# A two-layer decoder trunk: the order of row tiles in paired FFN blocks, the DRAM round trips of x, and the place of a bias table

## The chip, the cores and the metric

The kernel runs on one core of one Trainium2 chip. The metric is the device time of one launch in microseconds, for the slowest (here the only) core. Five engines work side by side, each through its own list of instructions in order, and wait for each other by semaphores: TensorE (PE, with its weight loads as PEld), VectorE (DVE), ScalarE (ACT), GpSimd (POOL) and SyncE (SP). DMAs are issued by SP and by POOL.

## The reference

For a sequence of 256 rows of width 2048, two layers run one after the other. Cut to what matters here:

```python
for i in range(2):
    h = rmsnorm(x, norm_mix[i])
    x = x + (even_mixer if i == 0 else odd_mixer)(h)      # attention-like heads and an output projection
    h = rmsnorm(x, norm_ffn[i])
    x = x + (silu(h @ ffn_gate[i]) * (h @ ffn_up[i])) @ ffn_down[i]          # inner width 5632
    x = x + sigmoid(x @ ple_gate[i]) * (p[i] @ ple_proj[i])                  # "ple" below
return rmsnorm(x, final_norm)
```

The odd mixer adds a bias to its logits, `t5_table[t5_bucket(distance)]`, one column for each of 16 heads. The kernel makes it once as a table `toep` of 128 x 16 x 256.

## The kernel before, in words

**Products.** Each weight matrix is read from DRAM in row tiles of 256 rows by 512 columns (512 KB; the tile `raw`). A row tile is split into two float32r parts: ACT writes the high part `whi` (L197), DVE subtracts it from the original to get the low part `wlo` (L199). The activations lie transposed in two big buffers, A and B, each with a high and a low part (`Ah`, `Al`, `Bh`, `Bl`). A plain row tile is 12 matmuls of 512 columns (lines 352, 353, 355: high times high, high times `wlo`, low times high, for two blocks of 128 rows of the weights and two halves of the sequence). Only the second of each three needs `wlo`.

**Pairs.** In the FFN two column blocks, a and b, are computed together. Four row tiles of the pair are replaced by seven "quads" of 6 matmuls each (lines 421 to 423), whose operands are sums of weight quarters (`e`, `keys`; added by DVE at L385) and sums of activations (`sums`, in the tile `tabs`). What is split there is split at L180 (ACT) and L182 (DVE). Some products land in a PSUM tile `at` and are combined by DVE (L431 to L435); when a block is finished DVE adds two such results to its accumulator (L441, L442, called close below). The order of work within a pair is a string: a digit is a quad, `a` or `b` a plain row tile of that block. In `"1a3a7a6a2aab5b4bbbb"`, quad 7 needs two DVE sums, quads 6 and 4 one each.

**The order of everything.** `run` walks through the list of row tiles. Before the products of row tile i it records the splits up to tile i+3 (`LOOK = 3`; four buffers for `whi` and `wlo`); after them, what becomes of a finished block; then one step of each background job that is due (`background`). One row tile is one tick. A job that yields `None, 7` is asked again 7 ticks later; `after=[...]` holds a job back until other jobs are done; `need` forces a job's steps when a product wants its result. DMA issues follow the same list. So all engines get their instructions in the order that this walk gives, and nothing is rearranged later by time.

**Turning x.** When a block of 512 columns of x is done (`add_x`, L613, then `after_x`), it has to be transposed into A or B for the next product. Blocks 0 to 2 go through DRAM: DVE transposes 32 x 32 squares (L541), POOL writes the tile `far` to DRAM (L543) and reads it back in another order (L546, four DMAs), and seven ticks later ACT and DVE split the result (L578 for the gains, L499, L500). Block 3 is transposed on PE (L513) and split from PSUM. Each block's job waits for the job of the block before. The hidden activations of the FFN (`hid`, made by DVE at L1164) take the same two ways.

**Stages of a layer.** Mixer, output projection (x blocks named xt1 in layer 0, xt4 in layer 1), FFN in three parts (gate and up for columns j0 to j1, then down for these; parts 0 and 1 have four j, part 2 has three), then ple (xt2, xt5 are the FFN's x for ple; xt3 is ple's x for the odd mixer). In part 2 the down pairs have 15 items; all other pairs have 19. After each FFN come four plain tiles of `ple_proj` and the blocks of `ple_gate`.

**The bias table.** `toep_steps` is a background job spawned after the FFN of layer 0: two small loads, one product of 16 x 384 on PE (L1034), a write of that result 32 times into DRAM (`dv`, L1039), and four DMAs of 512 KB that read it back skewed into the tile `tabs` (L1043), which takes over the place of `sums`.

Of the kernel before, what the change touches and what calls it, by code (L numbers as in the profile page):

```python
# [9 lines left out]
F32 = mybir.dt.float32  # L10
# [6 lines left out]
P = 128  # L17
S = 256
# [77 lines left out]
class Kernel:  # L96
# [501 lines left out]
    def after_x(self, cb, tag, dst, gain, squares=True, wait=1):  # L598

        if dst is not None:  # L600
            sums = ("sums", tag) if cb == 0 and tag in ("xt1", "xt4") else None
            self.spawn((tag, cb), self.xt_steps(cb, dst, gain, sums), after=[(tag, cb - 1)] if cb else (), kind="tp" if cb == 3 else None, wait=wait)
        if squares:
            self.spawn(("norm", cb), self.squares(cb), after=[("norm", cb - 1)] if cb else (), wait=wait)
            if cb == 0:
                self.done -= {("norm", c) for c in range(4)}
# [416 lines left out]
    def toep_steps(self):  # L1023

        nc = self.nc
        self.toep = self.const.tile([P, 16, S], F32, name="tabs")
        tab = self.sc.tile([33, 16], F32, name="tab", bufs=1)
        nc.vector.memset(tab[32:33, :], NEG)
        nc.gpsimd.dma_start(tab[:32, :], self.io["t5_table"])
        ohr = self.ring.tile([33, 384], F32, name="z", bufs=8)  # L1030
        nc.gpsimd.dma_start(ohr, self.io["ohr"])
        yield "at", 8
        at = self.ps.tile([P, 512], F32, name="at", bufs=2)
        nc.tensor.matmul(at[:16, :384], tab, ohr, start=True, stop=True)  # L1034
        vec = self.ring.tile([16, 384], F32, name="z", bufs=8)
        nc.scalar.activation(vec, at[:16, :384], AF.Copy)

        dv = self.dram.tile([16, 32, 384], F32, name="dv")
        nc.gpsimd.dma_start(dv, vec[:, None].to_broadcast([16, 32, 384]))  # L1039
        yield None, 3  # L1040
        for q in range(4):
            src = bass.AP(tensor=dv.tensor, offset=dv.offset + P - 1 - 32 * q, ap=[[383, 32], [32 * 384, 16], [1, S]])
            nc.gpsimd.dma_start(self.toep[32 * q:32 * q + 32], src)  # L1043
            if q < 3:
                yield None, 1
# [89 lines left out]
    def ffn(self, layer, src, mid, tag, tag2):  # L1135
        K, nc = self, self.nc
        hs = {}

        def evac_gate(blk):
            K.need([("norm", 3)])  # L1140
            sg = K.zt()
            for h in range(2):
                nc.scalar.activation(sg[:, h], blk.acc[h], AF.Silu, scale=K.rstd[:, h:h + 1])
            if blk.j == 10:
                K.table("sigmoid_and_others")
            hs[blk.j] = sg

        def hid_steps(j, k0, hid):
            if j == 10:
                yield from K.turn_fast(hid, mid, k0)  # L1150
                return
            t = K.turn_far(hid)
            yield None, 7
            K.split_far(t, mid, k0)
            if k0 == 0:
                yield None, 1
                for _ in K.sums_of(lambda k, h: K.far(t)[:, k:k + 2, h], K.sums[:, 1]):
                    yield None, 1

        def evac_up(blk):  # L1160
            sg = hs.pop(blk.j)
            hid = K.zt()
            for h in range(2):
                nc.vector.scalar_tensor_tensor(hid[:, h], blk.acc[h], K.rstd[:, h:h + 1], sg[:, h],  # L1164
                                               op0=OP.mult, op1=OP.mult)
            K.spawn(("hid", layer, blk.j), hid_steps(blk.j, (blk.j - blk.j0) * 4, hid),
                    kind="tp" if blk.j == 10 else None)

        def evac_down(blk):
            K.add_x(blk)  # L1170
            if blk.lastpart:
                K.after_x(blk.cb, tag2, src, None, squares=False)

        for p, (j0, j1) in enumerate(FFN_PARTS):
            for j in range(j0, j1):
                if j == 0:
                    self.blocks("ffn_gate", layer, j, 8, src, evac_gate, j=j,
                                needs=[[(tag, c // 2)] for c in range(8)])
                    self.blocks("ffn_up", layer, j, 8, src, evac_up, j=j, j0=j0)
                else:  # L1180
                    self.pair("1a3a7a6a2aab5b4bbbb", ("ffn_gate", "ffn_up"), layer, (j, j), 0, 8, src, 0, lambda: K.sums[:, 0],
                              (evac_gate, evac_up), lambda c: [("sums", tag)], j=(j, j), j0=(j0, j0))
            for c in range(0, 4, 2):
                if p == 2:
                    self.prog.append(("call", (lambda: K.load_p(layer)) if c == 0 else K.split_p))
                hid = lambda j: [("hid", layer, j // 2)]

                plan = (("1a3a7b6b2a5a4bb", "1a3a7a62a5b4bbb")[c // 2] if p == 2 else
                        ("1a3a7a6a2b5bbbaa4bb", "1a3a7a6a2aab5b4bbbb")[c // 2])
                self.pair(plan, ("ffn_down", "ffn_down"), layer, (c, c + 1), 2 * j0, 2 * (j1 - j0), mid, -4 * j0,  # L1190
                          lambda: K.sums[:, 1], (evac_down, evac_down), hid, cb=(c, c + 1), lastpart=(p == 2,) * 2)

# [178 lines left out]
    def build(self):  # L1371
        nc = self.nc
        self.setup()
        g = self.gains
        self.even_mixer()
        self.out_proj("w_out_even", self.B, [3, 2, 0, 1], "xt1", self.A, g[:, 0, 1])
        self.ffn(0, self.A, self.B, "xt1", "xt2")
        self.prog.append(("call", lambda: self.spawn("toep", self.toep_steps(), kind=None)))
        self.ple(0, self.A, "xt2", "xt3", self.B, g[:, 1, 0])
        self.odd_mixer()  # L1380
        self.out_proj("w_out_odd", self.A, [2, 3, 0, 1], "xt4", self.B, g[:, 1, 1])
        self.ffn(1, self.B, self.A, "xt4", "xt5")
        self.ple(1, self.B, "xt5", None, None, None)
        self.run()
# [55 lines left out]
```

## Time and profile before

| what | us |
|---|---|
| time, median of 3 runs | 2508.48 |
| lowest and highest of these | 2506.36, 2510.8 |
| time of the profiled execution | 2505.35 |
| its span, first to last instruction | 2503.6 |
| PE busy in the span | 2464.2 (98%) |
| DVE busy | 1859.0 (74%) |
| ACT busy | 1290.1 (52%) |
| granted clock of TensorE, mean | 0.997 |

The profile is of one execution, which took 2505.35 us; 1.75 us of it lie outside the span. That is 1.0 us below the lowest of the three runs and 3.1 us below their median. A matmul of 512 columns is shown with 0.39 us, but in a stretch without waits the next one starts 0.23 us later (they are pipelined), so PE can be shown busy while it loses time: the starts have to be compared, and not the busy shares. "clock" is 1.00 where TensorE was granted its full 2.4 GHz, 0.50 at 1.2 GHz.

### The profile page before, as it was taken

The numbers are of one execution on the slowest core, as the hardware profiler recorded it, in microseconds if no ns is written. First come the engines' busy times: TensorE is split into PE (matmuls) and PEld (weight loads), VectorE is DVE, ScalarE is ACT, GpSimd is POOL, SyncE is SP. The second block draws the span as 40 slices with busy tenths as digits, with TensorE's granted clock in tenths as the row PEclk, the third lists the DMA queues.
The fourth block names the chain that finished last, engine by engine and source line by source line (L and its number), as shares of the span: only waits on it lengthen the run. The fifth ranks groups of instructions, "written<-read, shape, count | busy, mean of one in ns | idle before, by whom it ended". The sixth has DMA issues, their size and how long they took to land.

```text
span 2503.6 us, 30924 instructions
## 1 busy us (share of the span) xinstructions
PE 2464.2 (98%) x11284; PEld 2025.7 (81%) x11284; DVE 1859.0 (74%) x2427; ACT 1290.1 (52%) x1701; POOL 141.7 (6%) x261
## 2 busy tenths in 40 slices
PE   8999999999999999999999999999999999999998
PEld 7888888787888878787789888878878887888787
DVE  5867766688888887888564666667888888888875
ACT  5444445555445554555453555565554555555554
POOL 0000001100000000101110000010000000000000
PEclk9999999999999999999999999999999999999999
DMA  7555557666656656666957435576666576657574
GB/s 272 189 173 182 178 176 224 219 231 202 212 194 222 228 199 219 198 221 211 246 179 235 133 127 168 160 235 217 212 210 218 193 243 202 221 183 240 178 242 137
DMA packets 146537, 508.70 MB, mean 203 GB/s; under 512 B 18037, under 2 KB 18549, under 8 KB 146256
## 3 DMA queue, kind: packets, MB, share of 16 engines
q1 hardware_dynamic: 132560, 464.25, 55.5%
q0 software_dynamic: 13392, 41.85, 6.1%
q8 instruction: 88, 1.44, 0.2%
q14 instruction: 65, 0.53, 0.1%
q10 hardware_dynamic: 432, 0.62, 0.1%
HBM read 485.42 MB, written 21.23 MB: 202 GB/s over the span
## 4 chain that ended last, share of the span: by engine, by line
PE 80%; DVE 12%; issue 4%; DMA 2%; ACT 2%; POOL 0%; SPq 0%; DVEq 0%; ACTq 0%; POOLq 0%
PE acc L353 23%; PE acc L355 22%; PE acc L352 22%; DVE wlo L199 3%; DVE wlo L182 2%; DVE e L385 2%; PE at L422 2%; PE at L421 2%; PE at L423 2%; PE acc L422 1%; PE acc L421 1%; PE acc L423 1%; ACT whi L180 1%; DVE z L1164 1%; DMA z<-far 1%
## 5 line engine op out<-in xcount | busy, mean ns | idle before, releaser
L199 DVE TENSOR_TENSOR wlo<-raw,whi 128x1024 fp32r<-128x1024 f32 (+3 forms) x753 | 895.7, 1193 | 412.9 <-ACT whi L197 410.6
L197 ACT ACTIVATE whi<-raw 128x1024 fp32r<-128x1024 f32 (+3 forms) x753 | 775.4, 1033 | 529.9 <-PE acc L355 458.3
L352 PE MATMUL acc<-whi,Ah 128*128 128x512 f32 (+1 forms) x1536 | 601.0, 391 | 10.6 <-ACT whi L197 8.8
L353 PE MATMUL acc<-wlo,Ah 128*128 128x512 f32 (+1 forms) x1536 | 596.7, 388 | 8.0 <-DVE wlo L199 6.9
L355 PE MATMUL acc<-whi,Al 128*128 128x512 f32 (+1 forms) x1536 | 594.9, 387 | 1.6 <-DVE Al L503 1.1
L352 PE MATMUL acc<-whi,Bh 128*128 128x512 f32 (+2 forms) x1440 | 558.7, 388 | 1.6 <-ACT Bh L499 1.6
L353 PE MATMUL acc<-wlo,Bh 128*128 128x512 f32 (+2 forms) x1440 | 553.8, 385 | 5.3 <-DVE wlo L199 4.5
L355 PE MATMUL acc<-whi,Bl 128*128 128x512 f32 (+2 forms) x1440 | 552.6, 384 | 0.7 <-DVE Bl L500 0.5
L353 PEld LDWEIGHTS acc<-wlo,Ah 128*128 128x128 f32 x1536 | 289.8, 189 | 77.4 <-DVE wlo L199 20.8
L352 PEld LDWEIGHTS acc<-whi,Ah 128*128 128x128 f32 x1536 | 289.8, 189 | 69.8 <-ACT whi L197 9.2
L355 PEld LDWEIGHTS acc<-whi,Al 128*128 128x128 f32 x1536 | 289.6, 189 | 61.6 <-DVE Al L503 2.1
L353 PEld LDWEIGHTS acc<-wlo,Bh 128*128 128x128 f32 x1440 | 271.1, 188 | 66.2 <-DVE wlo L199 15.6
L355 PEld LDWEIGHTS acc<-whi,Bl 128*128 128x128 f32 x1440 | 270.9, 188 | 55.0 <-DVE Bl L500 1.5
L352 PEld LDWEIGHTS acc<-whi,Bh 128*128 128x128 f32 x1440 | 270.9, 188 | 53.4 <-ACT Bh L499 1.9
L180 ACT ACTIVATE whi<-e 128x1024 fp32r<-128x1024 f32 x160 | 169.8, 1061 | 233.0 <-DVE e L385 157.2
L182 DVE TENSOR_TENSOR wlo<-e,whi 128x1024 fp32r<-128x1024 f32 x160 | 194.7, 1217 | 49.0 <-ACT whi L180 44.9
L385 DVE TENSOR_TENSOR e<-e 128x1024 f32<-128x1024 f32 x96 | 117.1, 1219 | 1.1
L543 POOL DMA_DIRECT2D far<-z x35 | 27.0, 771 | 1408.4 <-DVE z L541 1408.4
L180 ACT ACTIVATE whi<-keys 128x1024 fp32r<-128x1024 f32 x64 | 67.7, 1057 | 51.3 <-DVE keys L385 28.8
L182 DVE TENSOR_TENSOR wlo<-keys,whi 128x1024 fp32r<-128x1024 f32 x64 | 78.4, 1225 | 17.6 <-ACT whi L180 15.9
L546 POOL DMA_DIRECT2D z<-far x140 | 76.6, 554 | 142.0 <-DMA far<-z 59.3
L722 ACT ACTIVATE e<-e,m 128x128 f32<-128x128 f32 (+2 forms) x96 | 40.1, 419 | 75.5 <-DVE m L720 75.5
(298 smaller groups left out, 2184.6 us busy)
## 6 DMA issues: line engine op xcount, KB each, us to landing
raw<-in_ffn_gate SPq DMA_DIRECT2D x136, 512.0 KB, 4.2
raw<-in_ffn_up SPq DMA_DIRECT2D x136, 512.0 KB, 3.7
raw<-in_ffn_down SPq DMA_DIRECT2D x128, 512.0 KB, 4.1
raw<-in_w_in_even SPq DMA_DIRECT2D x103, 512.0 KB, 4.1
raw<-in_w_in_odd SPq DMA_DIRECT2D x80, 512.0 KB, 4.0
raw<-in_ple_gate SPq DMA_DIRECT2D x56, 512.0 KB, 5.0
e<-in_ffn_up SPq DMA_DIRECT2D x40, 512.0 KB, 4.6
e<-in_ffn_down SPq DMA_DIRECT2D x36, 512.0 KB, 4.8
```

What stands on the lines that cost most here:

```text
L180: nc.scalar.activation(hi, r, AF.Copy)
L182: nc.vector.tensor_tensor(lo, r, hi.bitcast(F32), op=OP.subtract)
L197: nc.scalar.activation(hi[:, c], r[:, c], AF.Copy)
L199: nc.vector.tensor_tensor(lo[:, c], r[:, c], hi[:, c].bitcast(F32), op=OP.subtract)
L352: nc.tensor.matmul(o, sh, wh, start=not self.started[h], stop=False)
L353: nc.tensor.matmul(o, sh, wl, start=False, stop=False)
L355: nc.tensor.matmul(o, sl, wh, start=False, stop=end)
L385: r, add = self.raw, lambda o, x: self.K.nc.vector.tensor_tensor(o, o, x, op=OP.add)
L421: nc.tensor.matmul(o, sh[:, i], wh, start=start and i == 0, stop=False)
L422: nc.tensor.matmul(o, sh[:, i], wl, start=False, stop=False)
L423: nc.tensor.matmul(o, sl[:, i], wh, start=False, stop=i == 1 and p in (1, 4, 5, 6, 7))
L546: nc.gpsimd.dma_start(back[32 * c:32 * c + 32].rearrange("p (q f) -> p q f", q=4), far[c].rearrange("(q i) f -> i q f", q=4))
```

## The change

Four edits:
1. The plans of the FFN pairs are other strings: each full pair begins with two plain row tiles (in part 2 with one), and the quads 1, 3, 2 come before 7, 6, 5, 4.
2. The x blocks no longer wait for the block before; blocks 0 and 1 start two ticks later than they otherwise would.
3. The job that turns the hidden activations starts two ticks later.
4. The bias table's job is spawned inside the FFN of layer 0, at part 1; it makes its product and the write to DRAM there, and waits for the label `ffn` before it reads the table back. Its two small tiles come from another pool (`pt` in place of `z`).

```diff
             sums = ("sums", tag) if cb == 0 and tag in ("xt1", "xt4") else None
-            self.spawn((tag, cb), self.xt_steps(cb, dst, gain, sums), after=[(tag, cb - 1)] if cb else (), kind="tp" if cb == 3 else None, wait=wait)
+            self.spawn((tag, cb), self.xt_steps(cb, dst, gain, sums), kind="tp" if cb == 3 else None,
+                       wait=wait + (2 if cb in (0, 1) else 0))
...
-        self.toep = self.const.tile([P, 16, S], F32, name="tabs")
...
-        yield None, 3
+        yield None, 3, (), ["ffn"]
+        self.toep = self.const.tile([P, 16, S], F32, name="tabs")
         for q in range(4):
...
+            yield None, 2
             t = K.turn_far(hid)
             yield None, 7
...
+            if layer == 0 and p == 1:
+                self.prog.append(("call", lambda: self.spawn("toep", self.toep_steps(), kind=None)))
...
-                    self.pair("1a3a7a6a2aab5b4bbbb", ("ffn_gate", "ffn_up"), layer, (j, j), 0, 8, src, 0, lambda: K.sums[:, 0],
+                    self.pair("aa1a3a2a7a6b5b4bbbb", ("ffn_gate", "ffn_up"), layer, (j, j), 0, 8, src, 0, lambda: K.sums[:, 0],
...
-                plan = (("1a3a7b6b2a5a4bb", "1a3a7a62a5b4bbb")[c // 2] if p == 2 else
-                        ("1a3a7a6a2b5bbbaa4bb", "1a3a7a6a2aab5b4bbbb")[c // 2])
+                plan = (("a1a3b2b7a6a54bb", "a1a3a2a7b6b54bb")[c // 2] if p == 2 else
+                        ("aa1a3a2b7b6b5baa4bb", "aa1a3a2a7a6b5b4bbbb")[c // 2])
...
-        self.prog.append(("call", lambda: self.spawn("toep", self.toep_steps(), kind=None)))
+        self.prog.append(("call", lambda: self.done.add("ffn")))
```

**Place one: DVE at the start of a pair.** The first two gate and up pairs meet here; L441 and L442 close the first, L1164 makes its hidden block, and what follows belongs to the second. Before:

```order
L442 TENSOR_TENSOR acc<-acc,z 128x512
L1164 SCALAR_TENSOR_TENSOR z<-acc,rstd,z 128x512 x2
L385 TENSOR_TENSOR e<-e 128x1024 x2
L199 TENSOR_TENSOR wlo<-raw,whi 128x1024
L541 STREAM_TRANSPOSE z<-z 128x4x4x32 x2
L182 TENSOR_TENSOR wlo<-e,whi 128x1024
L385 TENSOR_TENSOR e<-e 128x1024
L199 TENSOR_TENSOR wlo<-raw,whi 128x1024
```

The same place in the changed kernel (its L1166 is L1164 of before):

```order
L442 TENSOR_TENSOR acc<-acc,z 128x512
L1166 SCALAR_TENSOR_TENSOR z<-acc,rstd,z 128x512 x2
L199 TENSOR_TENSOR wlo<-raw,whi 128x1024
L182 TENSOR_TENSOR wlo<-e,whi 128x1024
L199 TENSOR_TENSOR wlo<-raw,whi 128x1024
L541 STREAM_TRANSPOSE z<-z 128x4x4x32 x2
L182 TENSOR_TENSOR wlo<-keys,whi 128x1024
L385 TENSOR_TENSOR e<-e 128x1024 x2
L199 TENSOR_TENSOR wlo<-raw,whi 128x1024
L182 TENSOR_TENSOR wlo<-e,whi 128x1024
L385 TENSOR_TENSOR e<-e 128x1024
```

The three weight sums (L385) stood directly behind the hidden block; now four splits and the transposes stand between.

**Place two: PE behind the FFN.** These are the first transposes (L513) of block 3 of xt2. Before, they stand among the `ple_gate` tiles, behind the fifth tile after the FFN:

```order
L352 MATMUL acc<-whi,Ah 128x512
L353 MATMUL acc<-wlo,Ah 128x512
L355 MATMUL acc<-whi,Al 128x512
L513 MATMUL tp<-ident,x 128x128 x4
L352 MATMUL acc<-whi,Ah 128x512
```

In the changed kernel the operand around them is the tile `z` (the split of `p`), so they stand among the `ple_proj` tiles, behind the first tile after the FFN:

```order
L352 MATMUL acc<-whi,z 128x512
L353 MATMUL acc<-wlo,z 128x512
L355 MATMUL acc<-whi,z 128x512
L513 MATMUL tp<-ident,x 128x128 x4
L352 MATMUL acc<-whi,z 128x512
```

They moved four tiles ahead; they read block 3 of x, which DVE adds last.

**Place three: POOL behind the FFN of layer 0.** Before, the table's DMAs stand between the last x block of the FFN and the first of ple:

```order
L543 DMA far<-z 128x4x256
L546 DMA z<-far 32x4x256 x4
L1029 DMA tab<-in_t_table 32x16
L1031 DMA z<-in_ohr 33x384
L1039 DMA dv<-z 512x1x384
L1043 DMA tabs<-dv 32x16x256 x3
L543 DMA far<-z 128x4x256
L546 DMA z<-far 32x4x256 x4
L1043 DMA tabs<-dv 32x16x256
```

In the changed kernel only the four reads are left there, and all of them stand ahead of the first x block of ple:

```order
L543 DMA far<-z 128x4x256
L546 DMA z<-far 32x4x256 x4
L1044 DMA tabs<-dv 32x16x256 x4
L543 DMA far<-z 128x4x256
L546 DMA z<-far 32x4x256 x4
```

The two small loads and the write to `dv` moved into the FFN's part 1.

## Rows read from the trace of the kernel before

**Rows 1.** The page: span, and busy time of each engine
```profile
span 2503.6 us, 30924 instructions
...
PE 2464.2 (98%) x11284; PEld 2025.7 (81%) x11284; DVE 1859.0 (74%) x2427; ACT 1290.1 (52%) x1701; POOL 141.7 (6%) x261
```

**Rows 2.** Windows of full pairs: length, busy us (x), then clock, DMA share, GB/s
```profile
485.08:527.56 42.48, 42.48 (x187) 34.90 (x186) 36.59 (x40) 23.67 (x25) 3.00 (x5) 1.00 0.66 218
527.56:570.81 43.25, 43.05 (x188) 34.75 (x186) 35.65 (x37) 22.71 (x24) 2.96 (x5) 1.00 0.68 224
...
700.53:743.19 42.66, 42.66 (x187) 34.82 (x186) 33.41 (x34) 22.00 (x23) 0.00 (x0) 1.00 0.59 198
```

**Rows 3.** Timeline of PE, into the sixth item of the second pair: start, us, instruction
```profile
537.33 0.40 PE L423 MATMUL at<-whi,tabs 128*128 128x512 f32 x1
537.56 0.40 PE L352 MATMUL acc<-whi,Ah 128*128 128x512 f32 x1
538.10 0.51 PE L353 MATMUL acc<-wlo,Ah 128*128 128x512 f32 x1
```

**Rows 4.** Timeline of DVE at the start of the same pair
```profile
528.53 1.40 DVE L1164 SCALAR_TENSOR_TENSOR z<-acc,rstd,z 128x512 f32<-128x512 f32 x2
529.84 2.48 DVE L385 TENSOR_TENSOR e<-e 128x1024 f32<-128x1024 f32 x2
...
533.37 1.30 DVE L541 STREAM_TRANSPOSE z<-z 128x512 f32<-128x512 f32 x2
...
536.83 1.22 DVE L199 TENSOR_TENSOR wlo<-raw,whi 128x1024 fp32r<-128x1024 f32 x1
```

**Rows 5.** Timeline of PE at the FFN's start in layer 0
```profile
448.77 0.60 PE L513 MATMUL tp<-ident,x 128*128 128x128 f32 x4
450.99 0.50 PE L352 MATMUL acc<-whi,Ah 128*128 128x512 f32 x1 [1.62 <-ACT Ah L499]
...
452.25 0.50 PE L355 MATMUL acc<-whi,Al 128*128 128x512 f32 x1 [0.53 <-DVE Al L500]
```

**Rows 6.** Timeline of POOL: writes of x blocks 0 and 2 (xt1)
```profile
392.96 0.84 POOL L543 DMA_DIRECT2D far<-z  x1 [40.94 <-DVE z L541]
...
433.73 0.76 POOL L543 DMA_DIRECT2D far<-z  x1 [12.22 <-DVE z L541]
```

**Rows 7.** Timeline of PE in ple of layer 0
```profile
1228.21 0.39 PE L355 MATMUL acc<-whi,Al 128*128 128x512 f32 x1
1231.62 0.50 PE L352 MATMUL acc<-whi,Ah 128*128 128x512 f32 x1 [3.03 <-ACT whi L197]
...
1236.55 0.44 PE L352 MATMUL acc<-whi,Ah 128*128 128x512 f32 x1
```

**Rows 8.** Timeline of ACT in ple of layer 0
```profile
1214.03 1.06 ACT L197 ACTIVATE whi<-raw 128x1024 fp32r<-128x1024 f32 x1 [3.31 <-DMA raw<-in_ple_gate]
...
1227.83 1.71 ACT L578 ACTIVATE z<-z,gains 128x256 f32<-128x256 f32 x4 [8.37 <-DMA z<-far]
```

**Rows 9.** Timeline of POOL in ple of layer 0
```profile
1198.95 1.97 POOL L1043 DMA_DIRECT2D tabs<-dv  x3 [9.56 <-PE acc L355]
```

**Rows 10.** Timeline of PE in the last down pair of layer 0
```profile
1127.56 0.40 PE L352 MATMUL acc<-whi,Bh 128*128 128x512 f32 x1
1130.22 0.50 PE L353 MATMUL acc<-wlo,Bh 128*128 128x512 f32 x1 [2.27 <-DVE wlo L199]
```

**Rows 11.** Windows: that wait, what follows, and both last down pairs
```profile
1127.90:1130.20 2.30, 0.05 (x1) 0.00 (x0) 2.26 (x2) 1.08 (x2) 1.36 (x3) 1.00 0.60 192
1130.80:1134.20 3.40, 3.40 (x10) 2.63 (x9) 3.33 (x4) 1.39 (x2) 0.00 (x0) 0.50 0.46 154
...
1088.57:1162.29 73.72, 70.81 (x302) 56.55 (x301) 68.85 (x78) 39.69 (x42) 6.67 (x11) 0.98 0.55 186
```

**Rows 12.** Timeline of PE and DVE where ple begins
```profile
1160.96 0.50 PE L352 MATMUL acc<-whi,z 128*128 128x512 f32 x1
...
1161.01 1.28 DVE L613 TENSOR_TENSOR x<-acc,x 128x512 f32<-128x512 f32 x2
```

More of the change, by code (lines that the diff above doesn't have):

```diff
@@ L1029, in toep_steps @@
         nc.gpsimd.dma_start(tab[:32, :], self.io["t5_table"])
-        ohr = self.ring.tile([33, 384], F32, name="z", bufs=8)
+        ohr = self.sc.tile([33, 384], F32, name="pt", bufs=self.SCRATCH["pt"])
         nc.gpsimd.dma_start(ohr, self.io["ohr"])
@@ L1034, in toep_steps @@
         nc.tensor.matmul(at[:16, :384], tab, ohr, start=True, stop=True)
-        vec = self.ring.tile([16, 384], F32, name="z", bufs=8)
+        vec = self.sc.tile([16, 384], F32, name="pt", bufs=self.SCRATCH["pt"])
         nc.scalar.activation(vec, at[:16, :384], AF.Copy)
```

## The prediction

> **What bounds the kernel now.** I read the busy shares first: PE is busy 2464.2 us of a span of 2503.6, DVE only 1859.0 [rows 1]. So PE sets the time, and a change that leaves its matmuls as they are can only win what PE loses between them. The busy share hides that: a matmul is shown with 0.40 us, but the next one starts 0.23 later when nothing holds it (537.33 and 537.56) [rows 3], so a wait of 0.3 us is only half seen as idle. I therefore compared starts of matmuls, first by windows of whole pairs, then by the timeline.
>
> Full pairs have equal work: 7 quads of 6 matmuls and 12 plain tiles of 12, 186 matmuls, by 0.227 us 42.2. The first pair of a layer follows plain blocks and takes 42.48. The second takes 43.25: 0.77 more [rows 2]. Of the 14 full pairs of a layer one is like the first row, two like the third (0.18 more) and eleven like the second. In both layers that is 22 by 0.77 and 4 by 0.18, **17.6 us**.
>
> The place of the loss is the fourth and the sixth item of the pair. The sixth starts at 537.56, and its second matmul, the first to read `wlo`, at 538.10 in place of 537.79, 0.31 late [rows 3]; the fourth loses about as much before it. DVE shows why: from 528.53 it works without a gap, hidden block, two weight sums, transposes, one more sum, and between them the splits, the last from 536.83 to 538.05 [rows 4]. At the pair's start PE has three tiles that were split ahead (two quads of 1.36 us and a plain tile of 2.72, 5.4 us); then it waits for DVE.
>
> Three larger losses stand by themselves. At the FFN's start PE does transposes at 448.77, then waits for the split of x block 2, and is through at 452.25 [rows 5]: 3.48 us for transposes of 0.36 and two matmuls (0.45), a loss of 2.67; layer 1 repeats it, together **5.3 us**. The blocks' jobs are a chain: block 0 is written at 392.96, block 2 only at 433.73 [rows 6]. In layer 0's ple PE starts 10 matmuls from 1228.21 to 1236.55, 8.34 us in place of 2.27, a loss of **6.1 us** [rows 7]; ACT stood 8.37 us before L578 for the DRAM read of an x block [rows 8], which was queued on POOL behind three table reads issued at 1198.95 [rows 9]. In the last down pair a matmul starts 2.66 us after the one before it in place of 0.23, 2.4 lost to a wait for `wlo` [rows 10]; the clock is 1.00 in the wait and 0.50, which is 1.2 GHz, in the 3.4 us after it [rows 11]. There a matmul takes 0.43 from start to start, so eight are done that need 1.8 at 2.4 GHz: 1.6 more.
>
> By the Trainium skill ("TensorE: Matmul & The Clock Gate", section "HAM oscillation — how this bites in real kernels") idle gaps send TensorE back to its slow clock, and each such gap pays anew. Rows 11 agree; it speaks against an edit that trades many short waits for a long one.
>
> **The change, part by part.** *Plans, and the hidden job's two ticks.* No matmul, split or sum is added; the order changes. Behind the hidden block DVE now has four splits and the transposes before any weight sum. From the last matmul of a pair on, by the durations in rows 4: close 1.2 and hidden block 1.3, 2.7 with the matmul's own latency; two splits of 1.15, 5.0; the next waits for its buffer (freed by PE at 5.6, ACT's half first) and is done at 7.9; transposes 9.1; split 10.2; two sums 12.6; the split for the plain tile before quad 7 13.7. PE reaches that tile after four plain tiles and three quads, at 15.0. So DVE is 1.5 us early at its tightest point, where before it was 0.3 late. The later quads (6, b, 5, b, 4) I laid out the same way: 1 to 2 us to spare, of which the sums of activations eat most once in each part. I take all 17.6 us as won. Bounds: no pair shorter than 42.48 is shown, so 17.6 is the upper end; if 0.3 stays in each pair, 9.
>
> *x blocks.* Block 2 is added 12 plain tiles, 33 us, before the FFN's fifth tile needs it. Without the chain its trip starts a tick or two later; in before it took from 433.73 to less than 450.99 [rows 5, 6], 17 us. So 5.3 won; at worst nothing. Block 3 is next: its transposes stand behind one plain tile of 2.72 us, its add takes DVE 1.3 among plain tiles that cost DVE 1.15 each, so it is not late there.
>
> *The end of the FFN.* There the same freedom costs. Block 3's transposes stood behind the fifth tile after the FFN; now they stand behind the first, and in PE's order all that follows waits with them for DVE's last add. From 1088.57, the start of the two last down pairs, to the end of that add at 1162.29 DVE is busy 68.85 of 73.72 us [rows 11, 12]: DVE bounds them, and the change gives it the same instructions there. PE's own work from 1088.57 to the end of the first `ple_proj` tile is 288 matmuls, 65.4, and 0.7 of transposes, 66.1. The last add can't end before 68.9, so PE must wait at least 2.8. Laid along DVE's new order it ends at 72.0, with some 2 us of waits inside the last pair and 3.5 at the transposes. Before, PE was at the second `ple_proj` tile at 1160.96, 72.4 after the start [rows 12]. Now it gets there at 72.0 and 0.4 of transposes, 72.4, the same; the slow clock after a wait longer than that of rows 10 costs 1.6, and 0.6 of transposes and small waits that came later before is gone: **1.0 us worse** in each layer, 2.0. Bounds: DVE at its 68.9 and no slow clock, 3.7 better per layer; DVE at 73.7 with it, 3 worse.
>
> *The table.* Its product and its copy on ACT only move. The write to `dv` now runs beside an FFN pair, where the DMA share is 0.66 [rows 2]; the product takes one `at` buffer for a moment between two quads. Both at nothing, hidden by the three tiles of lookahead; if a raw tile comes late in spite of it, 3.3 as in rows 8, once. The four reads are issued eleven ticks earlier, some 30 us, all ahead of ple's first x block, which is written eight plain tiles (21.8 us) behind the first of them. So the 6.1 go. What the reads can delay is weights: in rows 8 ACT waited 3.31 for a `raw` tile behind them, and PE did not, with three tiles in hand. Range 0 to 6.1.
>
> By the Trainium skill ("DMA: Bandwidth & Descriptors", "Issuing engines are not separate DMA queues") POOL's DMAs and SP's run on the same engines and interleave; the 3.31 us agree. Right behind the FFN, where PE has little in hand, that would be 3.3 lost, and the sum 23.7.
>
> Sum: 17.6 + 5.3 + 6.1 − 2.0 = **27.0 us**. The profiled execution (2503.6 span, 1.75 around it, 2505.35) would take 2478.4; it lies 3.1 below the median of the runs, which goes from 2508.48 to **2481.5**.
>
> **Rivals.** *The FFN's end does not wait.* With DVE at 68.9 and the clock up in both layers the ends give 7.4 in place of costing 2.0, in all 36.4: 2472. For it: 4.9 us of DVE are idle in rows 11. Against: they are waits for buffers that PE frees and for ACT.
>
> *The wait goes elsewhere in the pair.* If DVE, free of the sums at the start, is late at quad 7 or 5 by as much as it was at the start, the 17.6 stay and the rest gives 9.4: 2499. For it: the quads now alternate one to one with plain tiles to the end. Against: 1.5 us to spare by the rows' durations.
>
> *Slower.* The same place with a larger wait: quad 7's two sums wait for the last weight quarter, an `e` tile loaded nine items into the pair, and splits stand behind them on DVE. It decides where that load comes more than 1.5 us plus 1.0 late in each of the 28 full pairs: 28 are lost, all that is won. With waits as long as rows 10 and their slow clock, 4.0 in each, 112 are lost and 85 net: 2593. Against: the first pair in rows 2 makes the same sums two items earlier and loses nothing, at a DMA share of 0.66.
>
> *The change doesn't do what it says*: the table's reads still meet an x block or weights, or the chain's wait comes back where a product forces the job: 6 to 11 us less, 2488 to 2493.
>
> **How the numbers follow.** Forecast 0.72; the FFN's end free of waits 0.11; a collision left 0.08; the wait elsewhere 0.05; slower 0.04. The range goes down to 2467, the better ends and 5 us of short waits of 0.1 or less that no row counts, and up to 2495, with 9 in place of 17.6 and ends of 6 worse in place of 2; only the last two cases lie outside. About 0.2% (5 us) is what can be told from no change. Faster 0.94, within 0.02, slower 0.04: all cases but the slower one give 9 us or more, and a little is left for its small form.
>
> **What would show it.** Right: pairs of 42.5 us, and no `wlo` waits of PE at their fourth and sixth items; none at the FFN's start; none in ple of layer 0 after the last `ple_proj` tile; a wait of 2 to 4 us before the first L513 behind `ple_proj`, and clock 0.50 after it, in both layers. Wrong: pairs of 43.2 with the wait at a later item; ACT and then PE waiting for `raw` while the table is read; no wait at L513, and a time below 2475.

## The result, and the profile after

| | before | after |
|---|---|---|
| time, median, us | 2509.21 (2506.36 to 2510.8, 4 runs) | 2481.63 (2478.32 to 2481.91, 4 runs) |
| span of the profiled execution, us | 2503.6 | 2476.5 |

The ratio is 0.9888, 95% interval 0.9871 to 0.9905: 1.1% faster, clear of the noise. The profiled execution took 2478.32 us, the sum of the prediction said 2478.4. Executions of one kernel differ with the granted clock: of 19 executions of the kernel before that ran beside e1 to e4, those with a mean clock of 0.995 took 2510.8 to 2511.4 us, those with 0.998 took 2504.8 to 2505.4. So an agreement to 0.1 us is partly luck.

Where the 27.1 us of span went, from the starts of matmuls in both traces (each line is a stretch between the same two matmuls, by their number in PE's order):

| stretch | forecast | measured |
|---|---|---|
| 28 full pairs, without the table's product | −17.6 | −17.82 |
| the table's product and what follows it, in a pair and no longer in ple | 0 | +0.90 − 0.97 |
| both starts of the FFN | −5.3 | −5.36 |
| ple of layer 0 | −6.1 | −6.13 |
| both ends of the FFN | +2.0 | +2.74 |
| all else | 0 | −0.42 |

"Ends" here run from the start of part 2's first down pair to the end of the third `ple_gate` tile. The first pair won 0.93 in each layer, and the last pair with what follows lost 2.49 and 2.11.

The page, answering to [rows 1]:

```profile
span 2476.5 us, 30895 instructions
...
PE 2447.8 (99%) x11284; PEld 2028.3 (82%) x11284; DVE 1859.6 (75%) x2427; ACT 1299.7 (52%) x1701; POOL 143.3 (6%) x261
```

DVE does the same work in the same time; only its order is another. The windows of the first, second and sixth full pair, answering to [rows 2] (columns as there):

```profile
482.75:525.23 42.48, 42.48 (x188) 34.90 (x186) 36.32 (x39) 23.89 (x25) 3.01 (x5) 1.00 0.55 187
525.23:567.71 42.48, 42.48 (x188) 34.90 (x186) 36.10 (x38) 23.20 (x24) 2.96 (x5) 1.00 0.67 232
695.15:738.53 43.38, 43.38 (x190) 34.93 (x188) 33.49 (x35) 22.60 (x24) 0.65 (x1) 1.00 0.64 197
```

All full pairs but one take 42.48. The one with 43.38 holds the table's product (two more matmuls). DVE at the second pair's start, answering to [rows 4], and PE where DVE was forecast to have least to spare:

```profile
526.66 1.40 DVE L1166 SCALAR_TENSOR_TENSOR z<-acc,rstd,z 128x512 f32<-128x512 f32 x2
527.98 1.22 DVE L199 TENSOR_TENSOR wlo<-raw,whi 128x1024 fp32r<-128x1024 f32 x1
...
535.43 2.47 DVE L385 TENSOR_TENSOR e<-e 128x1024 f32<-128x1024 f32 x2
537.82 1.22 DVE L199 TENSOR_TENSOR wlo<-raw,whi 128x1024 fp32r<-128x1024 f32 x1
```

```profile
540.27 0.39 PE L352 MATMUL acc<-whi,Ah 128*128 128x512 f32 x1
540.50 0.39 PE L353 MATMUL acc<-wlo,Ah 128*128 128x512 f32 x1
```

The two sums are at 535.43 and no longer directly behind the hidden block. The split for the plain tile before quad 7 is done at 539.04, PE reads it at 540.50: 1.46 early, where 1.5 was forecast.

The FFN's start in layer 0, PE and POOL, answering to [rows 5, 6]:

```profile
440.97 0.60 PE L513 MATMUL tp<-ident,x 128*128 128x128 f32 x4
...
444.18 0.60 PE L513 MATMUL tp<-ident,x 128*128 128x128 f32 x4
...
445.08 0.40 PE L355 MATMUL acc<-whi,Al 128*128 128x512 f32 x1
```

```profile
398.75 0.84 POOL L543 DMA_DIRECT2D far<-z  x1 [46.38 <-DVE z L541]
...
407.11 0.76 POOL L543 DMA_DIRECT2D far<-z  x1
...
421.62 0.76 POOL L543 DMA_DIRECT2D far<-z  x1 [6.58 <-DVE z L541]
```

Block 2 goes out 23 us behind block 0, before 41, and PE has no wait there. In ple of layer 0 POOL and ACT, answering to [rows 8, 9]:

```profile
1158.18 2.60 POOL L1044 DMA_DIRECT2D tabs<-dv  x4
1198.36 0.78 POOL L543 DMA_DIRECT2D far<-z  x1 [37.58 <-DVE z L541]
```

```profile
1175.71 1.06 ACT L197 ACTIVATE whi<-raw 128x1024 fp32r<-128x1024 f32 x1 [3.83 <-DMA raw<-in_ple_gate]
...
1214.54 1.70 ACT L578 ACTIVATE z<-z,gains 128x256 f32<-128x256 f32 x4
```

All four table reads leave 40 us ahead of the x block, and L578 has no wait. ACT waits 3.83 for weights that came beside the reads, and no matmul starts late for it: the tiles split ahead cover it, as forecast.

The FFN's end is the one place that looks otherwise than forecast. PE from the last down pair to ple, then the windows of its waits and of what follows them, answering to [rows 10 to 12]:

```profile
1124.62 0.50 PE L353 MATMUL acc<-wlo,Bh 128*128 128x512 f32 x1 [0.98 <-DVE wlo L199]
...
1139.48 0.51 PE L352 MATMUL acc<-whi,Bh 128*128 128x512 f32 x1 [0.94 <-ACT whi L197]
1140.93 0.79 PE L353 MATMUL acc<-wlo,Bh 128*128 128x512 f32 x1 [0.95 <-DVE wlo L199]
...
1152.13 0.30 PE L513 MATMUL tp<-ident,x 128*128 128x128 f32 x1 [1.46 <-DVE x L614]
1152.64 0.55 PE L513 MATMUL tp<-ident,x 128*128 128x128 f32 x3 [0.21 <-DVE x L614]
```

```profile
1078.37:1152.59 74.22, 69.74 (x298) 55.73 (x296) 69.06 (x78) 38.09 (x41) 6.68 (x11) 0.98 0.58 187
...
1141.00:1144.00 3.00, 3.00 (x7) 2.41 (x8) 3.00 (x4) 1.27 (x2) 0.00 (x0) 0.50 0.63 202
1150.68:1152.13 1.45, 0.00 (x0) 0.03 (x1) 1.45 (x4) 0.00 (x0) 0.00 (x0) 1.00 0.94 254
1152.94:1155.56 2.62, 2.62 (x15) 2.16 (x14) 2.62 (x4) 1.81 (x3) 0.00 (x0) 1.00 0.74 264
```

The wait at the transposes is 1.7 (1.46 and 0.21) and not 3.5, and the clock stays at 1.00 after it; layer 1 shows the same, 1.38 and 0.20. The slow clock follows another wait, in the pair itself, that ACT began. POOL and ACT there:

```profile
1117.90 0.77 POOL L543 DMA_DIRECT2D far<-z  x1 [65.49 <-DVE z L541]
1122.25 2.20 POOL L546 DMA_DIRECT2D z<-far  x4 [3.58 <-DMA far<-z]
1124.45 0.77 POOL L543 DMA_DIRECT2D far<-z  x1
1131.75 2.19 POOL L546 DMA_DIRECT2D z<-far  x4 [6.53 <-ACT whi L180]
```

```profile
1137.42 1.06 ACT L499 ACTIVATE Ah<-z 128x1024 fp32r<-128x1024 f32 x1 [3.28 <-DMA z<-far]
1138.39 3.88 ACT L197 ACTIVATE whi<-raw 128x1024 fp32r<-128x1024 f32 x4
```

DVE behind that ACT instruction:

```profile
1138.52 1.23 DVE L500 TENSOR_TENSOR Al<-z,Ah 128x1024 fp32r<-128x1024 f32 x1 [1.79 <-ACT Ah L499]
```

x block 1 is written beside block 0's reads: 7.30 us from its issue to the issue of its own reads, where block 0 needed 4.35. By the trace the write itself landed 6.8 us after its issue, and block 0's 4.1 us after. (The row names ACT's L180 as the releaser; that can account for no more than the 0.5 us between the landing and the reads.) In e4, where block 1 goes out 6.6 us after block 0's reads began, its write landed after 3.5 us, which points to the neighbour as what slows it. So the data come late, ACT stands before L499, and four weight splits are queued behind it.

### The profile page after: what moved, and what is told of

It reads as the page before. It is cut to its first block, busy times and chain, and to the rows that moved or that the text cites. A ratio compares the mean times of both kernels' runs of the same rounds, so it can differ in the third digit from the quotient of the medians.

```text
span 2476.5 us, 30895 instructions
## 1 busy us (share of the span) xinstructions
PE 2447.8 (99%) x11284; PEld 2028.3 (82%) x11284; DVE 1859.6 (75%) x2427; ACT 1299.7 (52%) x1701; POOL 143.3 (6%) x261
## 4 chain that ended last, share of the span: by engine, by line
PE 94%; DVE 3%; DMA 1%; issue 1%; ACT 1%; POOL 0%; SPq 0%; POOLq 0%; DVEq 0%; ACTq 0%
PE acc L352 26%; PE acc L355 26%; PE acc L353 26%; PE at L422 2%; PE at L421 2%; PE at L423 2%; PE acc L422 2%; PE acc L421 2%; PE acc L423 2%; DVE wlo L199 1%; DMA raw<-in_w_in_even 1%; PE at L878 1%; DMA far<-z 0%; DVE z L530 0%; DMA z<-far 0%
## 5 line engine op out<-in xcount | busy, mean ns | idle before, releaser
L180 ACT ACTIVATE whi<-e 128x1024 fp32r<-128x1024 f32 x160 | 170.2, 1064 | 193.8 <-DVE e L385 104.1
L385 DVE TENSOR_TENSOR e<-e 128x1024 f32<-128x1024 f32 x96 | 117.0, 1219 | 1.1
L180 ACT ACTIVATE whi<-keys 128x1024 fp32r<-128x1024 f32 x64 | 67.8, 1059 | 33.9 <-DVE keys L385 25.4
```

The costliest lines, as they stand in the source:

```text
L180: nc.scalar.activation(hi, r, AF.Copy)
L385: r, add = self.raw, lambda o, x: self.K.nc.vector.tensor_tensor(o, o, x, op=OP.add)
```

## The experiments

Medians in us; each ratio is to the kernel before on the same chip, with its 95% interval. "The last stage" is the last down pair and what follows up to the end of the third `ple_gate` tile, by the starts of matmuls: 56.43 and 56.45 in the two layers before, 58.92 and 58.56 after. It differs between executions: in e7, e8 and e10 every engine has the changed kernel's instructions there, in the same order, and it took 58.7 to 60.5. So one figure for it is good to about 2 us. Without a wait it would be 52.1 (the pair's 32.06 in e4 and the rest's 20.01 in e2).

**e1, the plans alone.** The kernel before with the new strings and the two ticks.

> The kernel before with the new plans of the pairs and the hidden job's two ticks alone; x blocks chained, table behind the FFN. Theory (the parts stand by themselves): 24 of 28 full pairs become 0.75 shorter and 4 of them 0.18, 17.7 us; the waits at the hidden transposes at the start of part 2's first pair (1.0 per layer) go, since a plain tile stands ahead of them; in the last down pair 4.2 us of loss per layer become about 1.3, so 2.9 each. Sum 25.5 below before, near 2484. Rival (the pairs' gain needs the freed x blocks or the moved table, or the wait turns up at a later item): under 15 us, above 2494.

2493.49, ratio 0.9943 (0.993 to 0.9955): 9.5 more than the theory's sum, and nearly the rival's 2494, but not for the rival's reason. Full pairs are 42.48 but for one of 42.89, so they need neither of the other edits. The second pair:

```profile
527.98:570.46 42.48, 42.48 (x188) 34.91 (x186) 36.10 (x38) 23.18 (x24) 2.96 (x5) 1.00 0.68 237
```

But the last stage got longer, 59.19 and 57.86, in place of 2.9 shorter, and 2.0 more were lost in ple of layer 0, 1.6 more at layer 1's FFN start, the two places that the other edits mend. There the clock stood at 0.50 for longer than in the kernel before (1226.7 to 1233.4 us, and 1684.1 to 1687.4, where it had not fallen). PE at the second `ple_proj` tile:

```profile
1147.85 0.39 PE L355 MATMUL acc<-whi,z 128*128 128x512 f32 x1
1152.24 0.76 PE L352 MATMUL acc<-whi,z 128*128 128x512 f32 x1 [4.00 <-DVE x L613]
```

The x blocks are chained here and block 3's transposes stand five tiles later, and still PE waits 4 us for DVE's last add: the tile needs the accumulator that the add frees.

**e2, the freed x blocks alone.**

```diff
-... self.xt_steps(cb, dst, gain, sums), after=[(tag, cb - 1)] if cb else (), ... wait=wait)
+... self.xt_steps(cb, dst, gain, sums), ... wait=wait + (2 if cb in (0, 1) else 0))
```

> The kernel before with the x blocks freed of the chain alone; plans and table as before. Theory (the freed blocks win at the FFN's start, and cost at its end whatever the plan): 2.7 less at both starts, 5.4; at both ends 2 to 4 more, from ACT waiting for block 1's read from DRAM and PE waiting at block 3's transposes. Together 1.4 less to 2.6 more: no change that can be measured. Rival (the cost at the end comes from the new plans): 5.4 less, 2503.8.

2505.16, ratio 0.9988 (0.9979 to 0.9997). The time is 3 to 4 us less, between the two forecasts, and does not decide; the trace does. Both starts are 2.7 shorter, the last stage 3.9 and 2.9 longer (60.32, 59.39), as the theory had it. Not expected: in ple of layer 0 only about 2 of the 6.1 were still lost. The two ticks put weight splits ahead of ACT's L578, which waits 4.13 there and no longer 8.37.

**e3, the table alone.** `toep_steps` of the changed kernel, spawned in part 1.

> The kernel before with the table's job moved alone. Theory: ple of layer 0 loses 6.1 less, the product of 0.75 only moves: 2503.1. Rival (the early reads take the DRAM engines from weights or an x block there): 3.3 of it come back, 2506.4; or nothing is won.

2501.21, ratio 0.9973 (0.9963 to 0.9983). The 6.1 in ple went. Another 1.4 went in each layer's last pair, which the edit does not touch: the same wait as in [rows 10] stands there, but in the profiled execution the clock does not fall after it. The wait, then the stretch behind it:

```profile
1129.50:1131.80 2.30, 0.07 (x1) 0.00 (x0) 2.27 (x2) 1.07 (x2) 1.34 (x3) 1.00 0.67 196
1132.40:1135.80 3.40, 3.40 (x16) 2.81 (x15) 3.32 (x4) 1.84 (x3) 0.00 (x0) 1.00 0.44 154
```

The same two stretches in [rows 11] have 0.50 in the second.

**e4, block 1 later.** The changed kernel with

```diff
-                       wait=wait + (2 if cb in (0, 1) else 0))
+                       wait=wait + (2 if cb in (0, 1) else 0) + (3 if cb == 1 and tag in ("xt2", "xt5") else 0))
```

> The changed kernel with block 1 of xt2 and xt5 started three ticks later (its transposes, its DRAM trip and its split). Theory (the wait in the last pair comes from ACT, which stands 3.28 us at L499 for block 1's read from DRAM with the splits of weights queued behind it, because the write of block 1 goes out beside the reads of block 0): no ACT wait there, PE's losses of 4.0 and 3.7 us in the two layers go, the slow clock with them, and the 1.3 at the plain tile before quad 7 as well, since DVE's transposes of block 1 are later; some of it comes back at block 3's transposes, where PE still waits for the last add: 3 to 5 us less per layer, 2472 to 2476. Rival (DVE alone sets when the last add ends, so PE's wait only moves to those transposes): at most the slow clock, 1.6 per layer, 2478 or more.

2479.51, ratio 0.9886 (0.9873 to 0.99); span 2476.6 against 2476.5: no change, and the rival holds. The last pair has no wait longer than 0.4 (32.06 in place of 36.86), and the whole loss stands at the transposes, with the slow clock behind them. PE there, and DVE ahead of it without a gap:

```profile
1149.75 0.30 PE L513 MATMUL tp<-ident,x 128*128 128x128 f32 x1 [4.02 <-DVE x L614]
1150.26 0.55 PE L513 MATMUL tp<-ident,x 128*128 128x128 f32 x3 [0.21 <-DVE x L614]
```

```profile
1146.63 1.18 DVE L199 TENSOR_TENSOR wlo<-raw,whi 128x1024 fp32r<-128x1024 f32 x1
1147.73 0.69 DVE L441 TENSOR_TENSOR acc<-acc,z 128x512 f32<-128x512 f32 x1
1148.34 0.69 DVE L442 TENSOR_TENSOR acc<-acc,z 128x512 f32<-128x512 f32 x1
1148.93 1.27 DVE L614 TENSOR_TENSOR x<-acc,x 128x512 f32<-128x512 f32 x2
```

This is the picture the prediction drew for the changed kernel.

**e5, the last pair plain.** The changed kernel, with blocks 2 and 3 of the last down pair one after the other and without quads:

```diff
+                if p == 2 and c == 2:
+                    for cb in (2, 3):
+                        b = K.Block(K, mid, evac_down, k0=-4 * j0, cb=cb, lastpart=True)
+                        for ch in range(2 * j0, 2 * j1):
+                            K.mm("ffn_down", layer, (cb, ch), b, ch == 2 * j1 - 1, hid(ch))
+                    continue
```

> The changed kernel with the last down pair of part 2 done as two plain blocks, 12 plain tiles in place of 7 quads and 8 plain tiles: PE gets 6 matmuls more per layer (1.4 us), DVE loses three splits (1.2 each), three weight sums (1.2 each) and eight combining operations (0.7 each), some 13 us, and one block is finished six tiles before the other. Theory (DVE alone sets when the last add ends; e4 showed that the wait only moves): the losses of 6.8 and 6.4 us in the two layers, in the last pair, at block 3's transposes and by the slow clock, go but for 1 or less, and 1.4 is paid: 4 to 5 less per layer, 2472. Rival (the wait is for the DRAM trips of the freed blocks or for the transposes' place, and not for DVE's work): no more than the 1.3 at quad 7 goes and 1.4 is paid: 2481 to 2484.

2475.85, ratio 0.9873 (0.9858 to 0.9888): 4 to 6 us below the changed kernel, less than expected, and its interval overlaps that one's (0.9871 to 0.9905). The pair is free of waits, but 5.4 and 3.8 us are still lost at the first ple tiles, and DVE isn't what holds them: it stands idle, for ACT.

```profile
1145.73 1.23 DVE L500 TENSOR_TENSOR Al<-z,Ah 128x1024 fp32r<-128x1024 f32 x1 [7.59 <-ACT Ah L499]
```

```profile
1144.64 1.06 ACT L499 ACTIVATE Ah<-z 128x1024 fp32r<-128x1024 f32 x1 [7.76 <-DMA z<-far]
```

So two limits lie one behind the other: DVE's work, and behind it ACT's wait for block 1. Taking away one alone moves little.

**e6, the transposes later.**

```diff
+                       ... + (4 if cb == 3 and tag in ("xt2", "xt5") else 0))
```

> The changed kernel with block 3's transposes of xt2 and xt5 four ticks later, among the ple_gate tiles, where the kernel before had them. By the prediction (PE waits at the transposes because they stand ahead of the other ple_proj tiles): the wait of 2.0 us per layer in front of them goes and little comes in its place, 4 us less, 2477.6. Rival (PE would wait for the same add anyway, since the second ple_proj tile needs the accumulator that it frees, as in e1): the wait stands at that tile, no change, 2481.

2479.83, ratio 0.9889 (0.9874 to 0.9904); span 2476.4. The last stage is as in the changed kernel (58.42, 58.62). The wait stands at the second tile's accumulator:

```profile
1152.10 0.47 PE L352 MATMUL acc<-whi,z 128*128 128x512 f32 x1 [1.37 <-DVE x L614]
```

The rival holds: where the transposes stand makes no difference here.

**e7, the order of the quads alone**: full pairs `"1a3a2aa7a6ab5b4bbbb"` (the first down pair of a part `"1a3a2aab7b6b5baa4bb"`) in the changed kernel.

> The changed kernel with full pairs that have the new order of the quads (1, 3, 2 ahead of 7) but begin with quad 1, as before; the two plain tiles stand ahead of quad 7. Theory (what counts is that DVE's two sums for quad 7 stand behind more splits, so either half of the edit is enough): pairs stay at 42.5, 2481.6. Rival (the 6.8 us of work that PE has split ahead at a pair's start, two plain tiles and a quad, are needed): pairs are back at 43.2, 17.7 more, 2499.

2481.52, ratio 0.9897 (0.9881 to 0.9914). All full pairs take 42.48 (43.42 with the product). The second pair:

```profile
525.37:567.85 42.48, 42.48 (x188) 34.90 (x187) 35.72 (x37) 22.85 (x24) 2.95 (x5) 1.00 0.68 233
```

The two plain tiles ahead are not needed. The first sums (L385) stand behind three splits and the transposes here.

**e8, the two plain tiles alone**: full pairs `"aa1a3a7a62ab5b4bbbb"` (the first down pair `"aa1a3a7a62ab5bbb4bb"`).

> The changed kernel with full pairs that begin with two plain tiles but have the quads in the order of before (1, 3, 7, 6, 2, 5, 4; quads 6 and 2 without a plain tile between them). Theory (either half is enough): the start of a pair is free of waits, pairs of 42.5, 2481.6; if the neighbouring quads 6 and 2 make DVE late, some tenths each. Rival (the order of the quads is what counts): pairs of 43.2 with the wait at the fourth to sixth item, 2499.

2514.72, ratio 1.0029 (1.002 to 1.0038): slower than the kernel before. Yet the gate and up pairs and the second down pairs take 42.48 but for one of 43.07 and the one with the product (43.45), so this half is enough for them as well. The second pair, whose first sums stand behind two splits:

```profile
525.00:567.48 42.48, 42.48 (x188) 34.90 (x186) 35.63 (x37) 23.19 (x24) 2.95 (x5) 1.00 0.68 238
```

The time was lost elsewhere: in the four first down pairs, 50.4 to 51.5 each, since my string has all `a` tiles early and PE comes to the hidden block that was turned last before it is back from DRAM:

```profile
630.82 0.79 PE L352 MATMUL acc<-whi,Bh 128*128 128x512 f32 x1 [5.61 <-ACT Bh L499]
```

The plan of the change keeps two `a` tiles for the end there.

**e9, e5 with block 1's split later.**

```diff
-        yield None, 7
+        yield None, 11 if cb == 1 and gain is None else 7
         self.split_far(t, dst, 4 * cb, gain)
```

> The kernel of e5 with the split of x block 1 of xt2 and xt5 asked for 11 ticks after its DRAM trip in place of 7. Theory (what e5 has left, 5.4 and 3.8 us in its two layers at the first ple tiles, comes from ACT, which stands 7.76 us for block 1's read with the splits of the ple_proj weights queued behind it): no such wait, PE's losses there fall to 1 or less, 7 to 9 us less than e5: 2467 to 2469. Rival (DVE or the last add itself holds PE there): no change against e5, 2475.

2468.92, ratio 0.9846 (0.9829 to 0.9863), the best of all: its interval lies below the changed kernel's (0.9871 to 0.9905), and its time 10 to 13 us below. Three of its four runs took 2467.6 to 2469.1, the fourth 2476.11. The last stage takes 54.75 and 53.15 with 1.36 of PE work more. In layer 0 2.1 are left; there ACT stands 2.81 us before L499, now for block 2's read:

```profile
1153.08 1.06 ACT L499 ACTIVATE Ah<-z 128x1024 fp32r<-128x1024 f32 x1 [2.81 <-DMA z<-far]
```

The later split without the plain pair was not run; e4, which delays block 1 altogether, is the nearest to it.

**e10, without the hidden job's two ticks.**

> The changed kernel without the hidden job's two ticks, so that DVE's transposes of the hidden block stand two splits earlier. Theory (DVE has 1.5 us to spare at a pair's start and the transposes take 1.3): no change, pairs of 42.5, 2481. Rival (the ticks are needed): a wait of PE at the third to fifth item, 0.3 to 0.8 in each full pair, 2490 to 2503.

2479.94, ratio 0.9883 (0.9866 to 0.9899). Pairs stay at 42.48 (43.38 with the product): no change.

**e11, the table's job behind the FFN again**, the rest as changed.

> The changed kernel with the table's job where it was before, behind the FFN. By the prediction (the table's reads ahead of the x block's cost 6.1 in ple of layer 0, whatever else changes): 6.1 more, 2487.5. Rival (e2: the two ticks by which blocks 0 and 1 start later put weight splits ahead of ACT's wait for that read, so that the wait is covered without the move): no loss there, 2481.5.

2487.35, ratio 0.9912 (0.9897 to 0.9927). The loss in ple is back, 6.6 by the starts of matmuls, with ACT's wait:

```profile
1224.67 1.71 ACT L578 ACTIVATE z<-z,gains 128x256 f32<-128x256 f32 x4 [5.49 <-DMA z<-far]
```

The cover that e2 showed was not enough here; with the rest as changed, the move of the table earns its 6.

## Why the prediction was right, and where it wasn't

*Plans: right, in size and in cause.* 17.82 against 17.6, DVE 1.46 early against 1.5, and e1 shows the pairs free of waits with nothing else changed. The diff changes two things at once, and e7 and e8 show that either frees a gate and up pair: two or three splits between the hidden block and the first weight sums, where there were none, are enough. That the splits' number alone decides is not shown. The hidden job's two ticks were counted as nothing, and are (e10).

*x blocks at the start: right*, 5.36; e2 has it alone.

*The table: right*, 6.13, and 6.6 when it is undone (e11). The product cost the pair 0.90 and gave 0.97 back in ple. By the Trainium skill ("DMA: Bandwidth & Descriptors", section "Issuing engines are not separate DMA queues") transfers share the engines whoever issues them. The trace agrees (ACT's 3.83 above, before 3.31), and PE lost nothing, as the sum assumed; the sum of 23.7 us, with 3.3 lost to the table's reads, did not come.

*The FFN's end: the size about right, +2.74 for +2.0, and that by luck, since errors cancel; the place half wrong, and the cause incomplete.* Right was that DVE bounds the last two pairs, and e4 shows it best: waits taken out of the pair come back at the transposes. Three steps failed.

First, "some 2 us of waits inside the last pair and 3.5 at the transposes": 2.9 and 1.7 were measured in layer 0, and the sign "a wait of 2 to 4 us before the first L513 behind `ple_proj`, and clock 0.50 after it, in both layers" came in neither. I laid out DVE's order, and not the DRAM trips. Freed of the chain, block 1's trip meets block 0's, and ACT's 3.28 us wait for it holds four weight splits; PE waits 0.94 and 0.95 in the pair (0.55 and 0.95 in layer 1), and the slow clock follows there. DVE, too, then waits 1.79 for ACT, so its last add ended at 74.2 after the pairs' start, outside my bounds of 68.9 to 73.7 (73.8 in layer 1).

Second, "in PE's order all that follows waits with them". It waits anyway: the next tile needs the accumulators that the same add frees (e1, e6). So the loss was booked on the freed blocks alone, and the new plans bring it as well: e1 pays 2.8 and 1.4 with the chain kept, e2 pays 3.9 and 2.9 with the old plans, and both together pay 2.1 to 4.0 (the changed kernel and e7, e8, e10), hardly more than e2 alone. At this place the costs overlap and do not add. In ple of layer 0 parts interact too: the 4 us that e2 saved there are gone beside the new plans (e11). The times as a whole don't show it: e1 to e3 save 0.57, 0.12 and 0.27%, 0.96% in sum, and the whole change 1.12%, which the intervals don't tell apart.

Third, the transposes at the start of part 2's first pair were not looked at: a plain tile now stands ahead of them and their wait of 0.93 is gone in each layer. This and the two longer last stages (2.49 and 2.11, where 1.0 in each layer was forecast for the whole end) are errors of opposite sign.

*The slow clock* was priced at 1.6 once in each layer, and in the changed kernel it fell once in each; but where it falls was not foreseen, and in layer 0 of e1 and e2 it stood at 0.50 for over 6.7 us, about twice as long. By the Trainium skill ("TensorE: Matmul & The Clock Gate", section "HAM oscillation — how this bites in real kernels") idle gaps bring it. Here the same 2.3 us wait was followed by it in [rows 11] and not in e3, so the gap alone doesn't tell. It is a cost that comes or stays away, and a sum should carry it as a range.

The rivals: "the end free of waits" would have needed what e9 does; "the wait goes elsewhere in the pair" and the late `e` tile did not come, nor did a collision of the table's reads.

## What to carry to other kernels

Where one engine is the bound of a short stage, moving waits about in it changes nothing (e4, e6); take work from that engine, even if the other gets more of it, and then look for the next limit behind it (e5; e9 has both). Put long prerequisites of an in-order engine behind the short ones that others wait for: sums behind splits, and a split that waits for DRAM far enough behind its trip. Before adding up the parts of a change, ask which of them pay or save at the same place.

## What the runs showed of the hardware

The clock after a wait is not settled by the wait's length: 2.3 us of waiting in the same place were followed by 1.2 GHz in one kernel and by 2.4 GHz in another (e3). In the changed kernel it fell after two waits of 0.95 with one matmul between them, and not after one of 1.45. It differs between executions of the same instructions: in the last stage of layer 0 it stood at 0.50 within the pair in the changed kernel (1141.0 to 1144.0 us), and in e7 only behind the transposes (1153.5 to 1156.7). In the changed kernel's layer 0 a write of 512 KB to DRAM took 4.35 us from its issue to the issue of the reads that wait for it, and 7.30 beside another block's reads; in e4, away from these, 4.05 for the same block. In e5 it was 10.16.
